# FFN blocks of two token halves with the tokens stationary, ten raw weight buffers, copies on either of two engines, and a new order

## The chip, the cores and the metric

One Trainium2 chip; the kernel runs on one of its cores. The metric is the device time of one execution in microseconds (us), the median of three runs. Engines: PE multiplies matrices (PEld is its weight load), DVE is VectorE, ACT is ScalarE, POOL is GpSimd, SP issues the DMAs.

## The reference, cut to what matters

A trunk of two layers on 256 tokens of 1024 float32 channels. Each layer has a half-weighted SwiGLU block, a mixer with an output projection, and a second SwiGLU block, each followed by a LayerNorm. The mixer of layer 0 is an RWKV-7 recurrence, that of layer 1 is stick-breaking attention; a quarter of the heads attends to a fixed memory.

```python
def swiglu(x, w_gate, w_up, w_down):          # 1024 -> 2816 -> 1024
    return (jax.nn.silu(x @ w_gate) * (x @ w_up)) @ w_down
for i in range(DEPTH):
    x = layer_norm(ALPHA * x + 0.5 * swiglu(x, ffn1...[i]))
    proj = x @ (rwkv_w_in if i % 2 == 0 else sb_w_in)
    heads = concatenate([mixer(proj[..., :]), memory_attention(proj[..., -256:])])
    x = layer_norm(ALPHA * x + heads @ w_out[i])
    x = layer_norm(ALPHA * x + 0.5 * swiglu(x, ffn2...[i]))
```

## The kernel before, in words

The 256 tokens are two halves of 128, because the two mixers run half after half, while the other half's FFN work fills PE. Every large product is done in float32r with split operands: `piece` (L599) loads a 128x1024 piece of weights into a `raw` buffer by SP's queue, ACT rounds it to `hi`, and DVE subtracts to get `lo`; `mm3` (L627) then makes three matmuls out of one (hi by hi, hi by lo, lo by hi). There are 8 `raw` buffers and 9 each of `hi` and `lo`. A piece's `raw` buffer comes free when DVE has made its `lo`.

`ffn_block` (L737) does one block of 256 of the 2816 hidden channels: four pieces of gate and up weights, two pieces of down weights. A block is either for one half (a solo block) or for both (a shared block); `LAGS`, `spread` (L1393) and the calls from L1414 say which. Of the 44 blocks of the four SwiGLUs, 18 are shared (6, 2, 7 and 3). In a solo block the transposed tokens (`xTh`, `xTl`) are stationary and 512 columns of weights move; the hidden tile `h` comes out with tokens on the partitions and is turned by two PE transposes (`to_T`, L645), with the result split by ACT and DVE into `hT`. In a shared block the weights are stationary and 256 tokens move, so that `h` comes out turned already and is split without a transpose.

The order of all work is not the program's. `Plan` (L130) records each operation, prices it (`price`, L269), and `order` (L323) puts the operations into each engine's stream by a list schedule with priorities, buffers and engine clocks; `improve` (L508) repeats this with shaken priorities and keeps the best; `issue` (L536) writes the order out. Constants at L43 to L58 and L118 to L127 set the planner (`AHEAD`, `WAIT`, `SWITCH`, `TURN`, `BOOST`) and the sequence of blocks around the mixers (`HOLD`, `TAIL`, `LAGS`).

A plain copy has a fixed engine in the program: for example `put_back` (L1124) in the RWKV mixer writes one half of a small triangular inverse by ACT and the other by DVE, `mem_attention` (L830) copies the turned scores out of PSUM by DVE, and `stick` (L1281) does the same with scores of earlier tokens and with keys and values. Names in the rows: `ps_29r` and `ps_30r` are the PSUM banks of gate and up, `ps_25r` to `ps_28r` the accumulators of the two halves, `ps_2r` and `ps_3r` the banks of transposes and small products; `T`, `Tt`, `Y`, `lb`, `L`, `Lm` are 128x768 work tiles of the mixers, `Sk` and `qr` the scores in `stick`. All rows bear L562 (L599 in the changed kernel), the line that issues them.

Of the kernel before, what the change touches and what calls it, by code (L numbers as in the profile page):

```python
# [17 lines left out]
ALU = mybir.AluOpType  # L18
# [24 lines left out]
NRAW = 8  # L43
NPIECE = 9
# [60 lines left out]
class Op:  # L105
    __slots__ = ("i", "eng", "calls", "took", "lag", "after", "opens", "closes", "pri", "func", "port", "left", "ready",
                 "end", "users", "kb", "turns", "mode", "share", "spent", "fine", "parts", "round", "places")
# [19 lines left out]
TURN = 23520.0  # L127


class Plan:  # L130
# [56 lines left out]
    def add(self, eng, fn, method, a, k):  # L187
        if self.bundle and eng == "PE":
            o = self.bundle[0]
        else:  # L190
            o = Op()
            o.i, o.eng, o.calls, o.after, o.parts = len(self.ops), eng, [], {}, []
# [13 lines left out]
        return o  # L206

    def touch(self, o, x, w):
# [16 lines left out]
        if psum:  # L225
            for q in range(q0, q1):
# [7 lines left out]
                else:  # L234
                    if st["pe"][q] is not None:
                        dep[st["pe"][q]] = True
                    for j in st["epoch"][q]:
                        if j != o.i and self.ops[j].eng != o.eng:
                            dep[j] = True
# [29 lines left out]
    def price(self, o, method, aps, a, k):  # L269
# [5 lines left out]
        n = max(free(x) for x, _ in aps)  # L275
        if o.eng == "PE":
# [13 lines left out]
        elif o.eng == "ACT":  # L290
# [3 lines left out]
            o.took = 95.0 + 0.845 * n + 93.0 * ptr + (92.0 if "accum_out" in k else 0.0)  # L294
            o.lag = 95.0
        elif o.eng == "DVE":
# [5 lines left out]
            o.took = 75.0 + n / (1.92 if fast else 0.96) + 58.0 * (ptr > 0) * (n > 1)  # L302
# [20 lines left out]
    def order(self, given=()):  # L323
# [30 lines left out]
        mode, until, busy, cold = None, WINDOW, 0.0, True  # L354
        for o in ops:
            if not o.left:
                avail[o.eng].append(o)
# [11 lines left out]
        while done < len(ops):  # L369
# [5 lines left out]
            for e, c in () if given else clock.items():  # L375
                t_e, cand = None, []
                for o in avail[e]:
# [3 lines left out]
                    t = max(t, c)  # L381
                    cand.append((t, o))
# [19 lines left out]
            t, o = min((x for x in cand if x[0] <= t_e + ahead), key=rank)  # L402
            took = o.took
# [40 lines left out]
            avail[e].remove(o)  # L444
            for j in o.users:
                u = ops[j]
                same = u.eng == e
# [8 lines left out]
                if not u.left:  # L456
                    avail[u.eng].append(u)
# [3 lines left out]
        return out, [o.users for o in ops], soft, self.reuse, [o.spent for o in ops], max(o.end for o in ops)  # L461

    def latest(self, made):

        ops = self.ops
        out, links, soft, reuse, spent, end = made
# [14 lines left out]
        for o in ops:  # L481
            if not left[o.i]:
                avail[o.eng].append(o.i)
        for _ in ops:
# [9 lines left out]
            for j in need[i]:  # L494
# [3 lines left out]
                elif p.eng == e:  # L498
                    d = start[i] - (0.0 if e in ("PE", "SP") else p.lag + AGAIN * (e != "POOL"))
                else:  # L500
                    d = start[i] - LINK - (p.lag if p.eng != "SP" else 3500.0)
                due[j] = min(due[j], d)
                left[j] -= 1
                if not left[j]:
                    avail[p.eng].append(j)
        return start

    def improve(self):  # L508
# [3 lines left out]
        kept = dict(self.buffer), self.groups  # L512
        last, fails = best, 0
        for n in range(ROUNDS):
# [12 lines left out]
            if last[-1] < best[-1]:  # L527
                best, kept, fails = last, (dict(self.buffer), self.groups), 0
# [4 lines left out]
        self.buffer, self.value = kept[0], best[-1]  # L533
        return best[0]
# [31 lines left out]
def kernel(ctx, tc, const, x, mem, f1g, f1u, f1d, f2g, f2u, f2d, ln_g, ln_b, w_out, w_mem_kv,  # L566
# [32 lines left out]
    def piece(shape, *srcs):  # L599

        n = int(np.prod(shape))
        hi = new(wp, [P, D], F32R, "hi", "hi", NPIECE)[:, :n]
        lo = new(wp, [P, D], F32R, "lo", "lo", NPIECE)[:, :n]
# [133 lines left out]
    def ffn_block(w, c, halves, beside):  # L737
        gv, uv, dv = (m.rearrange("(k p) c -> p k c", p=P) for m in w)
        fs = slice(c * FC, (c + 1) * FC)
        alone = len(halves) == 1  # L740
# [26 lines left out]
        if alone:  # L767

            hf = halves[0]
            o = ps("gu")  # L770
            for k in range(KT):
                wh, wl = gu[k // 2]
                yield mm3(o, xT[hf][0][:, k], xT[hf][1][:, k], wh[:, k % 2], wl[:, k % 2], k == 0, k == KT - 1)
            h = new(tp_, [P, FC], F32, "ta", "h", 2)
            gated(h, o[:, :FC], o[:, FC:])

            def turn_h():
                hT = new(tp_, [P, 2, 2, P], F32R, "tb", "hT", 2)
                to_T(h, (hT[:, 0], hT[:, 1]), 0, 2)
                return [down(hf, hT[:, 0], hT[:, 1])]  # L780

            return turn_h

        o = [ps("gu") for _ in range(2)]
        for k in range(KT):
            for f in range(2):
                for u in range(2):
                    wh, wl = (t[:, k % 2, u * FC + f * P:u * FC + (f + 1) * P] for t in gu[k // 2])
                    b = o[f][:, u * SEQ:(u + 1) * SEQ]
                    with nc.together():  # L790
                        nc.tensor.matmul(b, wh, xTt[0][:, k], start=k == 0 and u == 0, stop=False)
                        nc.tensor.matmul(b, wh, xTt[1][:, k], start=False, stop=False)
                        nc.tensor.matmul(b, wl, xTt[0][:, k], start=False, stop=k == KT - 1 and u == 1)
            yield
        hT = new(tp_, [P, 2, 2, SEQ], F32R, "hT", "hT", NHT)
        for f in range(2):
            h = new(tp_, [P, SEQ], F32, "ta", "h", 2)
            gated(h, o[f][:, :SEQ], o[f][:, SEQ:])
            nc.scalar.activation(hT[:, 0, f], h, AF.Copy)
            nc.vector.tensor_sub(hT[:, 1, f], h, hT[:, 0, f].bitcast(F32))  # L800
        return lambda: [down(hf, hT[:, 0, :, half_sl(hf)], hT[:, 1, :, half_sl(hf)]) for hf in halves]
# [4 lines left out]
    def memory_kv():  # L806
# [5 lines left out]
        for g in range(2):  # L812
            mT = [new(wp, [P, D], F32R, n, "mT", NPIECE).rearrange("p (s k t) -> p s k t", s=NHALF, t=P) for n in ("hi", "lo")]
# [6 lines left out]
        for hf in range(NHALF):  # L820
            mk = new(tp_, [P, MEMW], F32, "ta", "mk", 2)
            nc.scalar.activation(mk, o[hf][:, :MEMW], AF.Copy)
# [655 lines left out]
```

## Time and profile before

| what | value |
|---|---|
| median of 3 runs | 1122.68 us (1121.04 to 1122.9) |
| the profiled execution, its own time | 1121.84 us |
| span of that execution's instructions | 1120.0 us |
| PE / PEld busy in the span | 96% / 80% |
| DVE / ACT busy | 84% / 66% |
| moved by DMA | 303 MB, mean 271 GB/s |
| mean granted PE clock | 0.989 |

How to read it: PE is nearly always busy by the profile, but ends of matmuls are modelled, so the times from start to start in the timeline tell more than its busy share. The span has stages: FFN of layer 0 to about 157 us, the RWKV mixer with FFN blocks beside it to about 490, FFN of both layers to about 770, the stick-breaking mixer to about 960, and the last FFN with the last two norms.

### The profile page before, as it was taken

Reading aid. Unit: us, or ns where it says so; the run is one execution under the profiler, and the core shown is the slowest. Engines: PE = TensorE matmul, PEld = TensorE weight load, DVE = VectorE, ACT = ScalarE, POOL = GpSimd, SP = SyncE. Lnnn points to the kernel's source line nnn. Section 1 sums busy time; section 2 is a strip of 40 time slices with the busy share of each in tenths; the row PEclk is TensorE's granted clock in tenths of the full one; section 3 lists DMA queues with packets and bytes.
Section 4 is the critical chain, followed back from the end, with each engine's and each line's share of the span. In section 5 each row is a group of like instructions: output and inputs, shape, how many; then the busy total and the mean of one; then the engine's idle time right before and its main releaser. Section 6 shows DMA issues by size and latency. Waiting matters only on the chain.

```text
span 1120.0 us, 19287 instructions
## 1 busy us (share of the span) xinstructions
PE 1072.2 (96%) x7057; PEld 900.9 (80%) x7057; DVE 944.5 (84%) x1357; ACT 734.0 (66%) x979; POOL 2.7 (0%) x14
## 2 busy tenths in 40 slices
PE   7999999998899889999999999999999999999996
PEld 6888887876668668788888889898877876888885
DVE  5667679999999999998879965658899999987777
ACT  6466557884259774576766654546787799766652
POOL 0000000000000000000000000000000000000000
PEclk9999999998999999999999999999999999999999
DMA  9598769764579577899989987676987996999883
GB/s 328 181 380 283 262 195 353 247 207 146 161 239 331 177 227 226 273 329 383 309 297 325 318 296 220 189 236 213 383 296 254 334 305 226 365 364 321 269 272 115
DMA packets 212257, 303.41 MB, mean 271 GB/s; under 512 B 13844, under 2 KB 159424, under 8 KB 212162
## 3 DMA queue, kind: packets, MB, share of 16 engines
q1 hardware_dynamic: 212162, 302.18, 80.3%
q8 instruction: 55, 0.90, 0.3%
q14 instruction: 40, 0.33, 0.1%
HBM read 301.08 MB, written 1.05 MB: 270 GB/s over the span
## 4 chain that ended last, share of the span: by engine, by line
PE 58%; DVE 11%; ACT 2%; issue 2%; DMA 2%; SPq 0%; DVEq 0%; ACTq 0%
PE ps_30r L562 17%; PE ps_29r L562 17%; PE ps_27r L562 6%; PE ps_28r L562 6%; PE ps_25r L562 4%; PE ps_26r L562 4%; PE ps_3r L562 2%; PE ps_2r L562 2%; DVE x L562 1%; DVE S_104r L562 1%; ACT L562 1%; DVE lo_41r L562 1%; DVE Y_351r L562 0%; DVE lb_480r L562 0%; DVE lo_14r L562 0%
## 5 line engine op out<-in xcount | busy, mean ns | idle before, releaser
L562 ACT ACTIVATE h_32r<-ps_30r 128x256 f32<-128x256 f32 (+1 forms) x49 | 20.6, 421 | 32.7 <-PE ps_30r L562 32.5
L562 ACT ACTIVATE h_33r<-ps_29r 128x256 f32<-128x256 f32 (+1 forms) x50 | 20.6, 412 | 23.4 <-PE ps_29r L562 22.3
L562 ACT ACT_TABLE_LOAD x17 | 21.8, 1283 | 1.0 <-PEq L1466 0.7
L562 PE MATMUL ps_30r<-hi_22r,xTh 128*128 128x512 f32 x50 | 20.9, 418 | 0.0
L562 PE MATMUL ps_30r<-lo_23r,xTh 128*128 128x512 f32 x50 | 19.6, 391 | 0.0
L562 PE MATMUL ps_30r<-hi_22r,xTl 128*128 128x512 f32 x50 | 19.5, 391 | 0.0
L562 DVE TENSOR_TENSOR h_32r<-h_32r,ps_30r 128x256 f32<-128x256 f32 x31 | 12.9, 417 | 7.6 <-ACT h_32r L562 7.4
L562 ACT ACTIVATE hi_19r<-raw_12r 128x1024 fp32r<-128x1024 f32 x13 | 13.8, 1060 | 6.8 <-PE ps_28r L562 3.0
L562 DVE TENSOR_TENSOR h_33r<-h_33r,ps_29r 128x256 f32<-128x256 f32 x32 | 13.3, 416 | 5.0 <-ACT h_33r L562 4.8
L562 DVE TENSOR_TENSOR lo_20r<-raw_12r,hi_19r 128x1024 fp32r<-128x1024 f32 x13 | 15.8, 1218 | 1.7 <-DMA raw_18r<-in_ffn_w_up_dram 1.6
L562 PE MATMUL ps_29r<-hi_34r,xTh 128*128 128x512 f32 x40 | 16.4, 411 | 0.7 <-DVE h_32r L562 0.7
L562 ACT ACTIVATE hi_37r<-raw_39r 128x1024 fp32r<-128x1024 f32 x11 | 11.6, 1056 | 8.2 <-DMA raw_39r<-in_rwkv_w_in_dram 6.4
L562 PE MATMUL ps_29r<-hi_7r,xTh 128*128 128x512 f32 (+1 forms) x42 | 16.2, 386 | 0.0
L562 PE MATMUL ps_29r<-lo_35r,xTh 128*128 128x512 f32 x40 | 15.8, 394 | 0.5 <-DVE lo_35r L562 0.5
L562 ACT ACTIVATE hi_34r<-raw_21r 128x1024 fp32r<-128x1024 f32 x11 | 11.6, 1058 | 7.0 <-DMA raw_21r<-in_rwkv_w_in_dram 2.8
L562 PE MATMUL ps_29r<-hi_7r,xTl 128*128 128x512 f32 (+1 forms) x42 | 16.0, 380 | 0.0
L562 PE MATMUL ps_29r<-lo_8r,xTh 128*128 128x512 f32 (+1 forms) x42 | 16.0, 380 | 0.0
L562 PE MATMUL ps_29r<-hi_34r,xTl 128*128 128x512 f32 x40 | 15.7, 392 | 0.0
L562 PE MATMUL ps_29r<-hi_19r,xTh 128*128 128x512 f32 x38 | 15.5, 407 | 0.0
L562 PE MATMUL ps_29r<-lo_20r,xTh 128*128 128x512 f32 x38 | 15.0, 395 | 0.4 <-DVE lo_20r L562 0.4
L562 PE MATMUL ps_2r<-cst,x 128*128 128x128 f32 x48 | 8.8, 313 | 6.8 <-DMA x<-in_x_dram 5.2
L562 DVE TENSOR_TENSOR lo_35r<-raw_39r,hi_34r 128x1024 fp32r<-128x1024 f32 x10 | 12.2, 1220 | 3.6 <-ACT hi_34r L562 3.6
(1913 smaller groups left out, 4456.3 us busy)
## 6 DMA issues: line engine op xcount, KB each, us to landing
raw_9r<-in_ffn_w_down_dram SPq DMA_DIRECT2D x26, 512.0 KB, 4.8
raw_39r<-in_ffn_w_gate_dram SPq DMA_DIRECT2D x41, 256.0 KB, 4.8
raw_39r<-in_ffn_w_up_dram SPq DMA_DIRECT2D x41, 256.0 KB, 5.1
raw_12r<-in_ffn_w_gate_dram SPq DMA_DIRECT2D x38, 256.0 KB, 5.6
raw_12r<-in_ffn_w_up_dram SPq DMA_DIRECT2D x38, 256.0 KB, 4.5
raw_24r<-in_ffn_w_gate_dram SPq DMA_DIRECT2D x38, 256.0 KB, 4.3
raw_24r<-in_ffn_w_up_dram SPq DMA_DIRECT2D x38, 256.0 KB, 4.9
raw_21r<-in_ffn_w_down_dram SPq DMA_DIRECT2D x18, 512.0 KB, 4.7
```

Source lines behind the costliest of these rows:

```text
L562: fn(*[at(x) for x in a], **{n: at(x) for n, x in k.items()})
```

## The change

Four things are changed. (1) A shared block is built like a solo block: tokens stationary, 512 columns of weights moving, once for each half, then two transposes for each half. The special `hT` buffer of shared blocks goes away. (2) `raw` has 10 buffers instead of 8. (3) `nc.copy` records a plain or scaled copy with two prices, and the planner puts it on ACT, or on DVE where ACT's clock is more than `SHY` = 1000 ns later than the time at which the copy could start; a term for strided operands is added to the price. (4) The planner's constants and two block counts (`HOLD`, `TAIL`) are other ones, so that the whole order differs.

```diff
-NRAW = 8
-NPIECE = 9
+NRAW = 10
+NHI = 9
+NLO = 9
-HOLD = (3, 4)
-NHT = 1
-TAIL = (1, 2)
-AHEAD = dict(PE=100.0, DVE=200.0, ACT=0.0)
-WAIT = 7.6832
-SWITCH = 68.6
-BOOST = 12.8625
+HOLD = (2, 4)
+TAIL = (2, 2)
+AHEAD = dict(PE=0.0, DVE=200.0, ACT=0.0)
+WAIT = 10.7565
+SWITCH = 192.08
+SHY = 1000.0
+BOOST = 18.0075
...
-TURN = 23520.0
+TURN = 47040.0
...
+    def copy(self, dst, src, scale=None):
...
+        o = self.add("ACT", self.real.scalar.activation, "activation", (dst, src, AF.Copy), k, True)
+        act = o.calls, o.took, o.lag, o.port
...
+        o.ways = dict(ACT=act, DVE=([call], o.took, o.lag, o.port))
...
+                    if o.ways and e == "DVE" and clock["ACT"] <= t + SHY:
+                        continue
...
+        far = 0.9 * n * any(len(x.ap) > 1 and x.ap[-1][0] >= 16 and x.ap[-1][1] > 1 for x, _ in aps)
...
-        if alone:
...
-        o = [ps("gu") for _ in range(2)]
-        for k in range(KT):
-            for f in range(2):
-                for u in range(2):
-                    wh, wl = (t[:, k % 2, u * FC + f * P:u * FC + (f + 1) * P] for t in gu[k // 2])
-                    b = o[f][:, u * SEQ:(u + 1) * SEQ]
-                    with nc.together():
-                        nc.tensor.matmul(b, wh, xTt[0][:, k], start=k == 0 and u == 0, stop=False)
...
+        o = {hf: ps("gu") for hf in halves}
+        for k in range(KT):
+            wh, wl = (t[:, k % 2] for t in gu[k // 2])
+            for hf in halves:
+                mm3(o[hf], xT[hf][0][:, k], xT[hf][1][:, k], wh, wl, k == 0, k == KT - 1)
+            yield
...
+                to_T(hs[hf], (hT[:, 0], hT[:, 1]), 0, 2)
...
-            nc.vector.tensor_copy(turned_e[-1], pt.rearrange("p (j m t) -> p j m t", j=2, m=2))
+            nc.copy(turned_e[-1], pt.rearrange("p (j m t) -> p j m t", j=2, m=2))
...
-                nc.scalar.activation(dst[:, :, BLK * b:BLK * b + BLK], src, AF.Copy, scale=quad[:, 0:1])
-                nc.vector.tensor_scalar(dst[:, :, 32 + BLK * b:32 + BLK * b + BLK], src, quad[:, 1:2], None, ALU.mult)
+                nc.copy(dst[:, :, BLK * b:BLK * b + BLK], src, quad[:, 0:1])
+                nc.copy(dst[:, :, 32 + BLK * b:32 + BLK * b + BLK], src, quad[:, 1:2])
...
-                        nc.vector.tensor_copy(zm[:, g], z[:, :384])
+                        nc.copy(zm[:, g], z[:, :384])
```

Three places of the order that the planner makes of it follow. The first is PE at the end of the gate and up products of the first shared block. Before, with a moving operand ahead of the stationary one in each row:

```order
L562 MATMUL ps_29r<-hi_37r,xTh 128x512
L562 MATMUL ps_29r<-lo_38r,xTh 128x512
L562 MATMUL ps_29r<-hi_37r,xTl 128x512
L562 MATMUL ps_30r<-xTh,hi_16r 128x256
L562 MATMUL ps_30r<-xTl,hi_16r 128x256
L562 MATMUL ps_30r<-xTh,lo_17r 128x256
```

and now:

```order
L599 MATMUL ps_30r<-hi_16r,xTh 128x512
L599 MATMUL ps_30r<-lo_17r,xTh 128x512
L599 MATMUL ps_30r<-hi_16r,xTl 128x512
L599 MATMUL ps_2r<-cst,h_31r 128x128 x2
L599 MATMUL ps_29r<-hi_37r,xTh 128x512
L599 MATMUL ps_29r<-lo_38r,xTh 128x512
L599 MATMUL ps_29r<-hi_37r,xTl 128x512
```

In the upper rows the last three products of the shared block (bank `ps_30r`) move the tokens, 256 columns at a time, between products of the next solo block; in the lower rows the weights move there too, 512 columns at a time, and the hidden tile `h_31r` of the shared block's first half is turned by two transposes of 128 columns.

The second place is ACT at `put_back` in the first half of the RWKV mixer, where the tiles `T` and `Tt` are written for the product that PE does next. Before:

```order
L562 ACTIVATE Y_351r<-Tt_340r,cst 128x16x16
L562 ACTIVATE lb_480r<-Tt_340r,cst 128x16x16
L562 ACTIVATE hi_34r<-raw_24r 128x1024
L562 ACTIVATE bn_416r<-ps_3r 128x256
L562 ACTIVATE T_350r<-Tt_340r,cst 128x12x16 x2
L562 ACTIVATE h_33r<-ps_29r 128x256
L562 ACTIVATE hi_10r<-raw_36r 128x1024
L562 ACTIVATE Tt_340r<-Y_351r,cst 128x12x16 x2
```

and now:

```order
L599 ACTIVATE Y_369r<-Tt_358r,cst 128x16x16 x2
L599 ACTIVATE lb_498r<-Tt_358r,cst 128x16x16 x2
L599 ACTIVATE hi_37r<-raw_39r 128x1024
L599 ACTIVATE T_368r<-Tt_358r,cst 128x12x16 x4
L599 ACTIVATE h_32r<-ps_29r 128x256
L599 ACTIVATE Tt_358r<-Y_369r,cst 128x12x16 x4
```

The four copies of each of `T` and `Tt` stood two on ACT and two on DVE; now all eight stand on ACT, and so do the copies of `Y` and `lb` ahead of them.

The third place is ACT in the second half of the stick-breaking mixer, where logarithms and exponentials alternate. Before:

```order
L562 ACT_TABLE_LOAD
L562 ACTIVATE L_356r<-L_356r 128x768
L562 ACT_TABLE_LOAD
L562 ACTIVATE T_350r<-T_350r 128x768
L562 ACT_TABLE_LOAD
L562 ACTIVATE Lm_341r<-Lm_341r 128x768
L562 ACTIVATE hi_13r<-raw_21r 128x1024
L562 ACTIVATE T_350r<-T_350r 128x768
L562 ACT_TABLE_LOAD
L562 ACTIVATE h_33r<-ps_29r 128x256
L562 ACTIVATE hi_22r<-raw_18r 128x1024
L562 ACT_TABLE_LOAD
```

and now:

```order
L599 ACT_TABLE_LOAD
L599 ACTIVATE Lm_359r<-Lm_359r 128x768
L599 ACTIVATE hT_1994r<-ps_3r 128x256
L599 ACTIVATE T_368r<-Sk_373r 128x768
L599 ACT_TABLE_LOAD
L599 ACTIVATE Lm_359r<-Lm_359r 128x768
L599 ACT_TABLE_LOAD
L599 ACTIVATE T_368r<-T_368r 128x768
L599 ACT_TABLE_LOAD
L599 ACTIVATE Tt_358r<-Tt_358r 128x768
L599 ACT_TABLE_LOAD
L599 ACTIVATE h_32r<-ps_30r 128x256
```

There are 17 table loads in the whole program before and 19 now; around this place it is 6 before and 8 now.

## Rows read from the trace of the kernel before

**Rows 1.** The page's first part: each engine's busy us, share of the span and number of instructions.

```profile
PE 1072.2 (96%) x7057; PEld 900.9 (80%) x7057; DVE 944.5 (84%) x1357; ACT 734.0 (66%) x979; POOL 2.7 (0%) x14
```

**Rows 2.** Three stretches: start and end in us, length, then busy us (and instructions) of PE, PEld, DVE, ACT, POOL, granted PE clock, DMA share, GB/s. The first two are the RWKV mixer, the third is the second half of the stick-breaking mixer.

```profile
196.00:308.00 112.00, 101.00 (x1130) 82.29 (x1129) 107.42 (x215) 68.69 (x114) 0.84 (x4) 0.95 0.59 191
308.00:476.00 168.00, 156.34 (x1357) 121.18 (x1357) 165.74 (x285) 110.45 (x164) 0.20 (x1) 0.99 0.76 246
896.00:952.00 56.00, 52.93 (x298) 39.49 (x297) 52.04 (x68) 52.63 (x68) 0.00 (x0) 1.00 0.81 265
```

**Rows 3.** The page's chain that ended last, shares of the span by engine.

```profile
PE 58%; DVE 11%; ACT 2%; issue 2%; DMA 2%; SPq 0%; DVEq 0%; ACTq 0%
```

**Rows 4.** Pieces of that chain in order of time: start us, length us, what, number of instructions.

```profile
314.91 4.90 DMA raw_21r<-in_rwkv_w_in_dram
...
394.95 3.44 DMA raw_15r<-in_ffn_w_gate_dram
...
463.98 3.42 DMA raw_9r<-in_ffn_w_gate_dram
467.51 3.97 DMA raw_36r<-in_ffn_w_gate_dram
...
503.88 5.48 PE ps_30r L562 x24
...
520.17 1.08 PE ps_29r L562 x9
...
888.64 4.50 DMA raw_12r<-in_ffn_w_up_dram
```

**Rows 5.** Timeline of PE: start us, length us, instruction, out<-moving,stationary. The pair of transposes is one row.

```profile
266.96 0.39 PE L562 MATMUL ps_27r<-hi_40r,hT_527r 128*128 128x512 f32 x1
267.19 0.38 PE L562 MATMUL ps_2r<-cst,h_32r 128*128 128x128 f32 x2
267.33 0.48 PE L562 MATMUL ps_28r<-hi_40r,hT_527r 128*128 128x512 f32 x1
267.64 0.40 PE L562 MATMUL ps_28r<-lo_41r,hT_527r 128*128 128x512 f32 x1
```

**Rows 6.** Groups of DVE instructions between 157 and 490 us, by shape: count, then busy us and mean ns of one, then idle time before them.

```profile
L562 DVE TENSOR_SCALAR Lm_341r<-ps_2r 64x384 f32<-64x384 f32 x3 | 1.6, 549 | 0.0
L562 DVE TENSOR_SCALAR Y_351r<-Tt_340r,cst 128x256 f32<-128x256 f32 x4 | 1.6, 398 | 0.0
...
L562 DVE TENSOR_SCALAR Tt_340r<-Y_351r,cst 128x192 f32<-128x192 f32 x4 | 1.4, 396 | 0.0
...
L562 DVE TENSOR_SCALAR T_350r<-Tt_340r,cst 128x192 f32<-128x192 f32 x4 | 1.3, 374 | 0.0
...
L562 DVE COPY L_356r<-ps_2r 128x384 f32<-128x384 f32 x2 | 1.1, 555 | 0.1
...
L562 DVE TENSOR_SCALAR mq_339r<-ps_3r 128x256 f32<-128x256 f32 x2 | 0.8, 420 | 0.0
...
L562 DVE TENSOR_SCALAR lb_480r<-Tt_340r,cst 128x256 f32<-128x256 f32 x2 | 0.7, 346 | 0.0
...
L562 DVE COPY pT_702r<-ps_2r 128x512 f32<-128x512 f32 x1 | 0.7, 689 | 0.0
...
L562 DVE COPY pT_373r<-ps_2r 128x512 f32<-128x512 f32 x1 | 0.7, 665 | 0.0
...
L562 DVE TENSOR_SCALAR Lm_341r<-ps_3r 64x384 f32<-64x384 f32 x1 | 0.6, 561 | 0.0
```

**Rows 7.** The same between 600 and 990 us.

```profile
L562 DVE COPY Sk_355r<-ps_28r 128x384 f32<-128x384 f32 x2 | 1.1, 554 | 0.1
...
L562 DVE COPY Sk_355r<-ps_27r 128x384 f32<-128x384 f32 x2 | 1.1, 548 | 0.0
...
L562 DVE COPY eT_1711r<-ps_3r 128x512 f32<-128x512 f32 x1 | 0.7, 692 | 0.0
```

**Rows 8.** Groups of ACT instructions of the whole span, by shape, with the same columns.

```profile
L562 ACT ACTIVATE hi_19r<-raw_12r 128x1024 fp32r<-128x1024 f32 x13 | 13.8, 1060 | 6.8 <-PE ps_28r L562 3.0 <-PE ps_29r L562 2.1 <-DVE mv_266r L562 1.1
...
L562 ACT ACTIVATE T_350r<-Tt_340r,cst 128x192 f32<-128x192 f32 x4 | 2.4, 640 | 0.4 <-DVE Tt_340r L562 0.4
L562 ACT ACTIVATE Tt_340r<-Y_351r,cst 128x192 f32<-128x192 f32 x4 | 2.3, 623 | 0.0
...
L562 ACT ACTIVATE Y_351r<-ps_3r 128x384 f32<-128x384 f32 x4 | 1.9, 484 | 2.0 <-PE ps_3r L562 1.7 <-ACT hi_37r L562 0.3
...
L562 ACT ACTIVATE pT_702r<-ps_2r 128x512 f32<-128x512 f32 x3 | 1.8, 594 | 0.6 <-PE ps_2r L562 0.6
```

**Rows 9.** Waits of PE between 224 and 476 us: who waited for whom, us in total, times, longest us.

```profile
PE ps_3r L562 <- DVE x L562: 5.1, 1, 5.1
PE ps_25r L562 <- ACT Tt_340r L562: 2.9, 1, 2.9
```

**Rows 10.** One stretch of the second stick-breaking half, with the columns of Rows 2.

```profile
917.00:933.00 16.00, 15.00 (x61) 10.67 (x59) 13.65 (x18) 15.84 (x17) 0.00 (x0) 1.00 0.66 245
```

**Rows 11.** Table loads of ACT in the same stretch, with the columns of Rows 6.

```profile
L562 ACT ACT_TABLE_LOAD x6 | 7.7, 1283 | 0.1
```

**Rows 12.** Timeline of ACT at the first of them: start us, length us, instruction.

```profile
917.04 1.28 ACT L562 ACT_TABLE_LOAD   x1
918.33 0.85 ACT L562 ACTIVATE L_356r<-L_356r 128x768 f32<-128x768 f32 x1
```

More of the change, by code (lines that the diff above doesn't have):

```diff
@@ L191, in add @@
             o = Op()
[L192 removed]
+            o.i, o.eng, o.calls, o.after, o.parts, o.ways = len(self.ops), eng, [], {}, [], {} if either else None
             o.pri = o.i + self.bias
@@ L402, in order @@
             t, o = min((x for x in cand if x[0] <= t_e + ahead), key=rank)
+            for n in o.ways or (o.eng,):
+                avail[n].remove(o)
+            if o.ways:
+                self.take(o, e)
             took = o.took
@@ L443, in order @@
                     heapq.heappush(free[self.tag_of[n]], (ends[n] + LINK, self.buffer[n]))
-            avail[e].remove(o)
             for j in o.users:
                 u = ops[j]
-                same = u.eng == e
+                same = u.eng == e and not u.ways
                 if o.i in soft[j]:
@@ L460, in order @@
         out.sort(key=lambda x: (x[0], x[1]))
-        return out, [o.users for o in ops], soft, self.reuse, [o.spent for o in ops], max(o.end for o in ops)
+        return out, [o.users for o in ops], soft, self.reuse, [o.spent for o in ops], [o.eng for o in ops], \
+            max(o.end for o in ops)
     def latest(self, made):
         ops = self.ops
-        out, links, soft, reuse, spent, end = made
+        out, links, soft, reuse, spent, eng, end = made
         finish = {o.i: t + spent[o.i] for t, _, o in out}
@@ L527, in improve @@
             if last[-1] < best[-1]:
-                best, kept, fails = last, (dict(self.buffer), self.groups), 0
+                best, kept, fails = last, (dict(self.buffer), self.groups, last[-2]), 0
             else:
@@ L533, in improve @@
         self.buffer, self.value = kept[0], best[-1]
+        for o in self.ops:
+            if o.ways:
+                self.take(o, kept[2][o.i])
         return best[0]
@@ L795, in ffn_block @@
[L795 to L801, printed above, removed]
+        o = {hf: ps("gu") for hf in halves}
[4 more added lines that the diff above has]
+            yield
@@ L803, with turn_h @@
+        hs = {}
+        for hf in halves:
+            hs[hf] = new(tp_, [P, FC], F32, "ta", "h", 2)
+            gated(hs[hf], o[hf][:, :FC], o[hf][:, FC:])
+        def turn_h():
+            res = []
+            for hf in halves:
+                hT = new(tp_, [P, 2, 2, P], F32R, "tb", "hT", 2)
+                to_T(hs[hf], (hT[:, 0], hT[:, 1]), 0, 2)
+                res.append(down(hf, hT[:, 0], hT[:, 1]))
+            return res
+        return turn_h
     memKT = cp.tile([P, 2, SEQ], F32, tag="memKT", name="memKT")
```

116 lines of the change are left out of this document (59 added, 57 removed).

## The prediction

> **What bounds the kernel now.** I read the page's engine totals first, then stretches of the span, then the chain of waits, then the shapes that the change touches. The totals [rows 1] show PE at 96% and DVE at 84%, but they are an average over stages with different limits. The stretches tell them apart [rows 2]: in the RWKV mixer, from 196 to 476 us, DVE is busy 107.42 + 165.74 = 273.2 of 280 us, while PE is busy 257.3 and so has at least 22.7 us without work. In that stage DVE is the limit. In the second half of the stick-breaking mixer, 896 to 952 us, ACT (52.63 of 56) and DVE (52.04) are level, and PE stands 3.1 us. Elsewhere PE is the limit: the chain that ended last lies 58% on PE, 11% on DVE, 2% on ACT and 2% on DMA [rows 3]. The work of DVE and ACT is mostly the rounding of weights (one hi on ACT is 1.06 us [rows 8]), which the change leaves alone; what can move is the rest.
>
> The sum is made against the profiled execution, 1121.84 us. The median of the runs is 0.84 us above it, and that is added at the end.
>
> **1. Shared blocks on PE.** 18 shared blocks have 96 matmuls of 256 columns each for gate and up: 1728 become 864 of 512 columns. From start to start, 9 narrow ones take 1.08 us, 0.120 each, and 24 wide ones 5.48 us, 0.228 each [rows 4]. So 207.4 us become 197.3: 10.1 us less. New are two transposes for each half of each block, 36 pairs. In the timeline of a pair between wide matmuls, the wide one at 266.96 and the one at 267.33 take 0.68 us to the start of the next at 267.64, with the pair between them [rows 5]; two wide ones alone are 0.46, so a pair costs 0.22, and 36 pairs 7.9 us. Net **-2.2 us**, all on PE, in stages where PE is the limit. If the wide ones go at the 0.23 to 0.235 of that timeline, the 864 take 198.7 to 203.0 us and the term is -0.8 to +3.5. On ACT and DVE the block costs the same: the hidden tile is split in as many instructions of 256 columns as before, from PSUM instead of SBUF. The two hidden tiles now wait in their two buffers until they are turned, and PE has the 24 down matmuls of the block before (5.4 us) to do meanwhile, so I cost that at nothing. Without this cover PE would wait in each block for about three instructions of 256 columns out of PSUM, 0.42 each by the row of mq [rows 6], 1.3 us, and 18 times that is 23 us.
>
> **2. Copies that leave DVE.** The order shows that 48 copies go from DVE to ACT and 2 the other way; only three copies of this kind are left on DVE. That "either engine" becomes, in effect, "ACT" is read off the order, not hoped for. Between 157 and 490 us the removed ones are [rows 6] Lm 1.6 + 0.6, Y 1.6, Tt 1.4, T 1.3, L 1.1, mq 0.8, lb 0.7 and four PSUM copies of 128x512 of about 0.68 each, 2.7: 11.8 us, less about 1.0 for the two that come. So 10.8 us leave an engine that is 98% busy there. The upper bound of the gain is 10.8. The lower one is 0: the order also moves a few more lo pieces in between the same norms, and part of the PE's idle time is waiting on a dependence, not on DVE's queue. Of the two long waits of PE in that stage, the one for the norm (DVE x, 5.1 us) [rows 9] stays: between the last sum and the last scaled row of that norm, DVE's list holds the same work as before. I take a little over half, **-6 us**, since DVE's load in rows 2 is nearer to a full queue than to a free one. In the stick-breaking mixer some 8.7 us more leave DVE (the scores Sk 1.1 + 1.1, four eT of 0.68 to 0.69 [rows 7], keys, values and queries), but ACT is as full there; nothing is taken for them.
>
> Here the Trainium skill speaks against the change. "ScalarE: Activation LUTs", section "Rules for kernel authors", says that cheap arithmetic belongs on VectorE and not on ScalarE, because VectorE is faster per element. The rows agree for strided copies within SBUF (128x192: 0.640 and 0.623 us on ACT [rows 8], 0.374 and 0.396 on DVE [rows 6]) and disagree for copies out of PSUM (128x512: 0.594 on ACT, 0.689 on DVE); by the rule alone term 2 would be a loss, and the first rival below is that case.
>
> **3. Ten raw buffers.** In the chain, five DMA landings lie on the path: 4.90, 3.44, 3.42, 3.97 and 4.50 us [rows 4], 20.2 in all. A transfer can start when DVE frees a raw buffer; two more buffers let it start up to two lo splits earlier. Five times two times about 1.1 us is 11 us, the upper bound; the lower is 0, because behind a late piece mostly stands the next busy engine. I take **-2 us**: these landings are the tail of a busy DVE more than of the queue. HBM traffic does not change.
>
> **4. Table loads and ACT's queue.** Two more table loads fall into the stretch where ACT is already 15.84 of 16 us busy [rows 10], six loads of 1.283 us among it [rows 11]. Two more are 2.6 us, and the scores' chain waits behind them: **+2.6 us**. In the trace the next activation starts 0.01 us after a load ends (917.04 + 1.28, then 918.33 [rows 12]), so the row is its whole price; the bound from below is 0, if PE has block work queued. The Trainium skill, "ScalarE: Activation LUTs", section "What ACT_TABLE_LOAD costs", gives about 2.66 us for each switch, a drain included; by that the term would be +5.3. The trace shows no such drain.
>
> **5. put_back and the new order.** In each half of the RWKV mixer four more strided copies stand on ACT ahead of the product that reads T and Tt: four times about 0.6 us, 2.4 longer on ACT, 4.8 in two halves. PE already waits 2.9 us there once [rows 9]. But the new order has 48 instead of 33 wide matmuls between the last masked product and that one (first half): 15 times 0.228 is 3.4 us of cover. Together I take **-2 us**, most of the one wait; bounds -2.9 and +4.8. The other constants of the planner only act through the order and get no term.
>
> Sum: -2.2 - 6 - 2 + 2.6 - 2 = -9.6; 1121.84 - 9.6 = 1112.2, and with 0.84 for the median **1113 us**.
>
> **The rivals.** *ACT becomes the bound* (ends slower). Its queue is in order, and copies now stand behind hi pieces of 1.06 us. Against it: ACT is busy 69 and 110 us of 112 and 168 in the RWKV mixer [rows 2]. For it: 94% in the second stick-breaking half. Price: put_back uncovered 4.8, loads 2.6, four Sk copies of 0.484 and two eT of 0.594 in that half 3.1 [rows 8], 10.5 in all, and none of terms 2 and 3; with -2.2 that is +8.3, **1131 us**. It decides where ACT is busy over 95% of the stick-breaking half and PE waits for Tt more than 5 us. The rule of the Trainium skill cited under term 2 ("ScalarE: Activation LUTs", "Rules for kernel authors") would act by this mechanism.
>
> *The path was not there.* The copies were hidden behind lo pieces that PE waits for anyway, and the chain of the mixer, not DVE's load, sets the stage: only term 1 is left, -2.2, **1120.5 us**.
>
> *The stage gives all of it.* DVE's 10.8, 11 from the landings, 2.9 from the wait, 2.2 from PE, less nothing for the loads: -26.9, **1096 us**. It needs DVE to be the one limit in the RWKV mixer from end to end; that PE already lacks only 22.7 us there speaks against so much.
>
> **How the numbers follow.** A measurement of this kernel can tell about 0.2%, 2.2 us, from no change. Forecast (1106 to 1119): 0.58. ACT as bound (1123 to 1135): 0.13. No path (1118 to 1123): 0.17, of which 0.13 are the same and 0.02 each side. All of it (1091 to 1104): 0.12. Faster is 0.58 + 0.12 + 0.02 = 0.72, the same 0.13, slower 0.13 + 0.02 = 0.15. The range goes from 1099 to 1127: it leaves out the lower half of the large gain and the upper part of the ACT case, some 0.15. As both signs hold little between them, the forecast's own range is the 1106 to 1119 above.
>
> **What would show it.** Step 1: wide matmuls in shared blocks at 0.227 to 0.235 from start to start; 36 more pairs of transposes. Step 2: DVE's busy total down by some 20 us to about 925, and the stretch between the first norm and the third norm's end shorter, with PE's idle time in it below 18 us. Step 3: less than 20 us of DMA in the chain. Step 4: 19 table loads, eight in the second stick-breaking half, and that half not shorter. Step 5: PE's wait for Tt under 2 us. The prediction is wrong if the RWKV stretch keeps its length with DVE less busy, or if the time goes or comes in the pure FFN stages, where I see 2 us.

## The result, and the profile after

The changed kernel takes **1110.32 us** (median of 4 runs, 1109.82 to 1111.31), the kernel before 1122.79 (4 runs): a ratio of 0.9894, 95% interval 0.9876 to 0.9911. That is 12 us less, where 10 were forecast. The profiled execution has a span of 1108.5 us against 1120.0.

Engine totals of the changed kernel, against [rows 1]: PE is busy 4 us less, DVE 16 less, ACT 26 more.

```profile
PE 1068.3 (96%) x6265; PEld 862.6 (78%) x6265; DVE 928.6 (84%) x1312; ACT 760.0 (69%) x1027; POOL 2.7 (0%) x14
```

To see where the time went, the span is cut at points that mean the same in every order: the end of PE's last transpose behind a norm. The two stretches that matter are the whole RWKV mixer, from the first norm's transposes to the fourth's, and the second half of the stick-breaking mixer. The columns are those of [rows 2]. First the kernel before:

```profile
164.50:503.60 339.10, 316.05 (x2760) 250.77 (x2758) 329.13 (x576) 223.65 (x331) 1.04 (x5) 0.98 0.74 243
890.60:990.90 100.30, 97.23 (x505) 75.99 (x503) 94.41 (x127) 86.82 (x115) 0.00 (x0) 1.00 0.91 311
```

And the changed one:

```profile
162.30:490.40 328.10, 312.50 (x2767) 251.60 (x2766) 317.00 (x548) 237.90 (x363) 1.05 (x5) 0.98 0.76 251
876.00:980.80 104.80, 99.79 (x510) 78.13 (x509) 90.50 (x119) 92.45 (x124) 0.00 (x0) 0.97 0.84 294
```

The RWKV mixer is 11.0 us shorter with 12.1 us less on DVE; PE stands 15.6 us in it instead of 23.1. The second stick-breaking half is 4.5 us **longer**. By the same cuts the rest gives 2.2 us before the mixer, 1.4 between the two stretches (1.1 in the FFN of both layers, 0.3 in the first half of the stick-breaking mixer) and 1.4 at the end: 11.0 + 2.2 + 1.4 + 1.4 - 4.5 = 11.5, the difference of the spans.

Pieces of the chain, against [rows 4]: wide matmuls go at 5.47 / 24 = 0.228 us, and five DMA landings lie on the path inside the RWKV mixer, 16.1 us of them. They can't be set against [rows 4] as they stand: the chain of the kernel before could be followed back only to 271 us (its shares in [rows 3] add up to 75% of the span), that of the changed kernel to the start. From 271 us on the mixer has 15.7 us of landings on the path before and 6.7 now, the last two below.

```profile
218.13 2.58 DMA raw_48r<-in_ffn_w_gate_dram
239.69 3.56 DMA raw_42r<-in_ffn_w_gate_dram
256.95 3.29 DMA raw_18r<-in_w_out_dram
412.00 2.67 DMA raw_21r<-in_ffn_w_up_dram
470.71 4.00 DMA raw_24r<-in_ffn_w_up_dram
490.65 5.47 PE ps_30r L599 x24
```

PE's timeline at two pairs of transposes, against [rows 5]: from 646.91 to 647.82 are 0.91 us for two wide matmuls (0.456) and two pairs, 0.227 a pair.

```profile
646.91 0.39 PE L599 MATMUL ps_28r<-hi_7r,hT_876r 128*128 128x512 f32 x1
647.15 0.38 PE L599 MATMUL ps_3r<-cst,h_32r 128*128 128x128 f32 x2
647.36 0.38 PE L599 MATMUL ps_2r<-cst,h_31r 128*128 128x128 f32 x2
647.50 0.48 PE L599 MATMUL ps_29r<-hi_19r,xTh 128*128 128x512 f32 x1
647.82 0.40 PE L599 MATMUL ps_29r<-lo_20r,xTh 128*128 128x512 f32 x1
```

Waits of PE between 157 and 505 us, against [rows 9]: the wait for the norm has stayed (6.1 us in this wider window before), the one for Tt has shrunk from 2.9 to 0.4 us.

```profile
PE ps_2r L599 <- DVE x L599: 7.0, 2, 5.7
...
PE ps_26r L599 <- ACT Tt_358r L599: 0.4, 1, 0.4
```

The loss in the second stick-breaking half is to be read in the chain of waits, against [rows 10 to 12]:

```profile
909.68 1.28 ACT L599
...
910.97 0.84 ACT Lm_359r L599
...
911.84 1.28 ACT L599
...
913.13 0.84 ACT T_368r L599
...
913.99 1.28 ACT L599
...
915.29 0.85 ACT Tt_358r L599
...
916.16 0.96 DVE Tt_358r L599
917.12 0.47 DVE qr_408r L599
...
917.64 1.65 PE ps_2r L599 x2
```

The pieces without a name are table loads: one stands ahead of nearly every activation, since Ln (Lm, Tt) and Exp (T) alternate. DVE's add for Tt waits for the last of them; behind it in DVE's queue stands the subtraction for qr, which frees the PSUM buffer that PE wants. PE waits 5.0 us for it, and then runs at the lower of its two clock levels for a while. In the two stretches below the granted clock (third column from the end) is 0.74 while PE is nearly idle and 0.63 while it is busy again, before it is back at 1.00 (923 to 928 us).

```profile
912.00:918.00 6.00, 0.99 (x3) 0.37 (x3) 2.37 (x4) 5.91 (x7) 0.00 (x0) 0.74 0.00 0
918.00:923.00 5.00, 5.00 (x14) 3.47 (x14) 2.96 (x6) 4.11 (x5) 0.00 (x0) 0.63 0.00 0
```

Three wide matmuls of PE's timeline there stand 0.43 us apart, from start to start:

```profile
919.94 0.63 PE L599 MATMUL ps_26r<-hi_10r,hT_1994r 128*128 128x512 f32 x1
920.36 0.63 PE L599 MATMUL ps_25r<-hi_10r,hT_1994r 128*128 128x512 f32 x1
920.79 0.63 PE L599 MATMUL ps_25r<-lo_11r,hT_1994r 128*128 128x512 f32 x1
```

### The profile page after: what moved, and what is told of

Its sections match the earlier page's. It is cut to its first block, busy times and chain, and to the rows that moved or that the text cites. A ratio compares the mean times of both kernels' runs of the same rounds, so it can differ in the third digit from the quotient of the medians.

```text
span 1108.5 us, 17727 instructions
## 1 busy us (share of the span) xinstructions
PE 1068.3 (96%) x6265; PEld 862.6 (78%) x6265; DVE 928.6 (84%) x1312; ACT 760.0 (69%) x1027; POOL 2.7 (0%) x14
## 4 chain that ended last, share of the span: by engine, by line
PE 79%; DVE 11%; ACT 4%; DMA 3%; issue 2%; SPq 0%; DVEq 0%; ACTq 0%
PE ps_30r L599 25%; PE ps_29r L599 23%; PE ps_27r L599 7%; PE ps_28r L599 6%; PE ps_25r L599 6%; PE ps_26r L599 6%; PE ps_2r L599 3%; PE ps_3r L599 3%; DVE x L599 1%; DVE Y_369r L599 1%; DVE lo_44r L599 1%; DMA raw_21r<-in_ffn_w_up_dram 1%; DVE lo_17r L599 1%; ACT L599 1%; DVE lb_498r L599 1%
## 5 line engine op out<-in xcount | busy, mean ns | idle before, releaser
L599 ACT ACT_TABLE_LOAD x19 | 24.4, 1283 | 1.1 <-PEq L1488 0.7
L599 PE MATMUL ps_30r<-hi_10r,xTh 128*128 128x512 f32 (+1 forms) x60 | 23.6, 393 | 0.0
L599 PE MATMUL ps_30r<-hi_10r,xTl 128*128 128x512 f32 (+1 forms) x60 | 23.0, 383 | 0.0
L599 PE MATMUL ps_30r<-lo_11r,xTh 128*128 128x512 f32 (+1 forms) x60 | 22.9, 382 | 0.0
L599 PE MATMUL ps_29r<-hi_16r,xTh 128*128 128x512 f32 x56 | 22.8, 407 | 0.0
L599 PE MATMUL ps_30r<-hi_13r,xTh 128*128 128x512 f32 x54 | 22.0, 408 | 0.0
L599 PE MATMUL ps_29r<-hi_16r,xTl 128*128 128x512 f32 x56 | 21.9, 391 | 0.0
L599 PE MATMUL ps_29r<-lo_17r,xTh 128*128 128x512 f32 x56 | 21.9, 391 | 0.0
L599 PE MATMUL ps_30r<-lo_23r,xTh 128*128 128x512 f32 x56 | 21.8, 390 | 0.0
L599 PE MATMUL ps_30r<-lo_14r,xTh 128*128 128x512 f32 x54 | 21.2, 392 | 0.4 <-DVE lo_14r L599 0.4
L599 PE MATMUL ps_30r<-hi_13r,xTl 128*128 128x512 f32 x54 | 21.2, 393 | 0.0
L599 PE MATMUL ps_29r<-hi_10r,xTh 128*128 128x512 f32 x52 | 21.2, 408 | 0.0
```

What stands on the lines that cost most here:

```text
L599: fn(*[at(x) for x in a], **{n: at(x) for n, x in k.items()})
```

## The experiments

Two kinds of edits were made. In the first, **the order is kept**: the changed kernel's plan is made as it is, and only then one thing is altered, so that PE, SP and all other work stand in the same sequence. In the second, the planner makes a new order for the edit. All times are medians; the last column is (ratio - 0.9894) x 1122, against the changed kernel. By the intervals of the two ratios such a difference is known to about 2.4 us.

| run | order | us | ratio to before, 95% | RWKV mixer / 2nd stick half, us | against the change, us |
|---|---|---|---|---|---|
| the change | | 1110.32 | 0.9894 (0.9876 to 0.9911) | 328.1 / 104.8 | |
| copies_rwkv_back | kept | 1119.05 | 0.9974 (0.9963 to 0.9984) | 337.9 / 105.1 | +9.0 |
| copies_all_back | kept | 1121.48 | 0.9995 (0.9986 to 1.0003) | 336.3 / 107.7 | +11.3 |
| strided_back | kept | 1113.94 | 0.9928 (0.9915 to 0.9942) | 331.7 / 104.6 | +3.8 |
| raw_8 | kept | 1124.73 | 1.0024 (1.0014 to 1.0034) | 341.8 / 106.1 | +14.6 |
| shared_256 | kept | 1120.47 | 0.9992 (0.9983 to 1.0001) | 330.1 / 104.3 | +11.0 |
| ln_after_exp | all but ACT's kept | 1105.44 | 0.9853 (0.9840 to 0.9865) | 328.1 / 98.8 | -4.6 |
| copies_fixed_replanned | new | 1113.38 | 0.9922 (0.9909 to 0.9935) | 338.1 / 97.3 | +3.1 |
| raw_8_replanned | new | 1117.51 | 0.9959 (0.9947 to 0.9971) | 331.0 / 103.3 | +7.3 |
| old_planner_numbers | new | 1116.80 | 0.9950 (0.9939 to 0.9962) | 336.4 / 101.9 | +6.3 |
| shared_blocks_alone | new | 1118.03 | 0.9957 (0.9943 to 0.9971) | 336.9 / 101.2 | |
| other_seed | new | 1110.39 | 0.9894 (0.9880 to 0.9907) | 327.4 / 105.2 | 0.0 |
| loads_priced | new | 1103.59 | 0.9831 (0.9818 to 0.9845) | 328.1 / 96.5 | -7.1 |

**copies_rwkv_back, copies_all_back, strided_back.** Each copy carries the engine that it had before; after the planning, the copies go back to it. The bound 3000 on the operation's number keeps this to the RWKV mixer; copies_all_back is without it, and strided_back has a second one, that the copy writes Y, lb, T or Tt.

```diff
         for o in self.ops:
             if o.ways:
                 self.take(o, kept[2][o.i])
+        for o in self.ops:
+            if o.ways and o.i < 3000:
+                self.take(o, o.was)
```

> The changed kernel with its order kept instruction for instruction on PE, SP and in time; only the 30 copies of the RWKV mixer (and two beside it) that the change took from DVE to ACT go back to DVE at the same place in the order, and one pT copy back to ACT. Theory (DVE is the limit of that mixer, its load decides): the 10.8 us return to DVE and cost about +6 us against the changed kernel, so 1116 to 1117; bounds +3 to +11. Rival A (the gain of that mixer comes from the new order and from PE's own work, not from the engine of the copies): within 2 us of 1110. Rival B (every us of DVE counts): +10.8 or more, 1121. Seen in the trace: PE's idle time between the first norm and the transposes of the fourth goes from 15.5 us to 21 or more by the theory, stays at 15 to 17 by rival A.

> As copies_rwkv_back, and the 17 copies of the stick-breaking mixer go back to DVE as well. Theory (they were hidden, ACT being as full as DVE there): the same time as copies_rwkv_back within 2 us. Rival (DVE is the limit there too): their 8.7 us come on top in good part, +4 to +9 against copies_rwkv_back. A third way: ACT gets its 9 us back in the second stick-breaking half and that half becomes shorter, -2 to -4 against copies_rwkv_back.

> The changed kernel with its order kept and only the 14 copies within SBUF of the RWKV mixer's inverse (Y, lb, T, Tt, all but two of them strided) back on DVE, where each takes about 0.37 us in place of 0.64; the eight of put_back are among them. Theory (DVE is the limit of that mixer, so its 5.0 us more count in the share that the run copies_rwkv_back showed, 8.8 of 10.8): +3 to +5 us against the changed kernel, 1113 to 1115. Rival (these copies stand on the chain of the inverse, one behind the other on ACT, and cheap arithmetic belongs on the faster engine): -1 to -3, since put_back is 1.2 us shorter for each matrix with two engines, 1107 to 1109.

The mixer's copies cost 9.0 us, between the theory's +6 and the bound of 10.8; rival A falls. The stretch of copies_rwkv_back shows it one to one:

```profile
162.80:500.70 337.90, 316.12 (x2765) 252.79 (x2765) 328.07 (x577) 225.65 (x334) 1.05 (x5) 0.98 0.75 244
```

DVE is busy 11.1 us more and the stretch is 9.8 longer, with PE idle for 21.8 us. The copies of the stick-breaking mixer add 2.3 us, at the edge of the "same time" that was expected; PE's wait behind the table loads grows from 5.0 to 6.1. strided_back settles the rule on the faster engine. On DVE these copies are shorter, as the groups of that run show (mean ns of one behind the busy us):

```profile
L603 DVE TENSOR_SCALAR Y_369r<-Tt_358r,cst 128x256 f32<-128x256 f32 x4 | 1.6, 390 | 0.0
L603 DVE TENSOR_SCALAR Tt_358r<-Y_369r,cst 128x192 f32<-128x192 f32 x4 | 1.6, 390 | 0.0
L603 DVE TENSOR_SCALAR T_368r<-Tt_358r,cst 128x192 f32<-128x192 f32 x4 | 1.5, 386 | 0.0
L603 DVE TENSOR_SCALAR lb_498r<-Tt_358r,cst 128x256 f32<-128x256 f32 x2 | 0.7, 350 | 0.0
```

They are 5.4 us on DVE by this sum (DVE's busy time in the mixer grows by 3.9, from 317.0 to 320.9), the mixer is 3.6 us longer and the kernel loses 3.8: the engine that is slower for the single copy is the better one, because the other is full.

**raw_8.** The loads take eight buffers in turn; a load is issued only when the lo split of the piece eight places ahead of it stands in DVE's queue before it. `fewer` puts out each engine's list unchanged and holds a load back until a buffer is free.

```diff
-        return best[0]
+        return self.fewer(best, 8)
```

> The changed kernel with 8 raw buffers in place of 10 and the order of every engine kept; only each load waits for the buffer of the eighth piece before it. Theory: +2 us, 1112 (bounds 0 and +4): two buffers let a load start two lo splits earlier, and what is late then is DVE and not the queue. Rival A (no landing was bound by the buffers): 0, 1110. Rival B (the order is planned for ten buffers, and each of the mixers' stretches runs dry): +8 or more, 1118 and above, with DMA landings of over 30 us in the chain.

Rival B holds in time and sign: +14.6 us, 13.7 of them in the RWKV mixer, with 59.8 us of DMA landings in the chain from about 280 us on, where the change has 13.9. In the mixer it is 29.5 us, 24.4 of them weights, against 6.7. One of these landings shows a way that neither text had:

```profile
454.68 1.23 DVE lo_41r L632
...
456.90 5.05 DMA T_368r<-in_rwkv_lnx_g_dram
...
461.97 0.96 DVE T_368r L632
```

SP's timeline shows what the transfer of this gain, of the mixer's own norm, stood behind:

```profile
451.26 0.46 SPq L632 DMA_DIRECT2D raw_24r<-in_ffn_w_up_dram  x1
455.93 0.37 SPq L632 DMA_DIRECT2D raw_39r<-in_ffn_w_gate_dram  x1
456.35 0.46 SPq L632 DMA_DIRECT2D raw_39r<-in_ffn_w_up_dram  x1
456.90 0.43 SPq L632 DMA_DIRECT2D T_368r<-in_rwkv_lnx_g_dram  x1
```

The weight load for `raw_39r` waits 4.1 us for the lo split, and the gain, next in SP's list, goes out behind it, though DVE had read `T` for the last time by 449.7 us. DVE then waits for its landing (from the lists of SP's waits from 445 to 460 us and DVE's from 338 to 505; us in total, times, longest):

```profile
SPq L632 <- DVE lo_41r L632: 4.1, 1, 4.1
...
DVE T_368r L632 <- DMA T_368r<-in_rwkv_lnx_g_dram: 3.3, 1, 3.3
```

So DVE, the full engine, stands for a transfer that its own queue had delayed. This is one place, 3.3 of the 13.7 us; the others were not followed one by one.

**shared_256.** Each 512-column matmul of a shared block is issued as two of 256.

```diff
+                    if o.cut:
+                        out, st, mv = [at(x) for x in a]
+                        fn(out[:, :256], st, mv[:, :256], start=k["start"], stop=False)
+                        fn(out[:, 256:], st, mv[:, 256:], start=False, stop=k["stop"])
+                        continue
```

> The changed kernel with each of the 864 matmuls of 512 columns of the shared blocks' gate and up cut into two of 256 columns, at the same place in the order. Theory (PE is the limit wherever a shared block runs, and a narrow one goes each 0.120 us against 0.228): 864 x 0.012 = +10.4 us, 1120.7; by the 0.230 of other rows +8.6. Rival (the shared blocks lie in stretches where DVE or the loads set the pace): +3 or less, PE's busy share rising and its idle time falling by the rest.

The narrow ones go each 0.120 us, and +11.0 is the +10.4 of the theory. It falls where the shared blocks lie: +3.8 us before the RWKV mixer, +4.7 between the two stretches, +1.5 at the end, while the mixer and the second stick-breaking half, which have none, change by +2.0 and -0.5. PE's busy sum is 8.6 us larger and its idle time no smaller, against the rival.

```profile
699.76 0.28 PE L603 MATMUL ps_29r<-hi_40r,xTh 128*128 128x256 f32 x1
699.88 0.28 PE L602 MATMUL ps_29r<-lo_41r,xTh 128*128 128x256 f32 x1
700.00 0.28 PE L603 MATMUL ps_29r<-lo_41r,xTh 128*128 128x256 f32 x1
```

**ln_after_exp.** On ACT alone, the four Ln of the second stick-breaking half move behind the last Exp of the scores.

```diff
+        lns = [x for x in act if x[2].func == "Ln"][2:]
+        last = max(n for n, x in enumerate(act) if x[2].func == "Exp" and x[0] < lns[-1][0])
+        lines["ACT"] = [x for x in act[:last + 1] if x not in lns] + lns + [x for x in act[last + 1:] if x not in lns]
```

> The changed kernel with one thing moved: in the second half of the stick-breaking mixer the four Ln of ACT stand together behind the last Exp of the scores, in place of between them; six ACT table loads fewer, every other engine's order kept. Theory (term 4: the loads are on the path; DVE's add for Tt waits for the fifth load's Ln, and behind it in DVE's queue stands the subtraction that frees the PSUM buffer that PE waits 5.0 us for, after which PE runs some 4 us at the lower clock): the wait goes and with it the slow matmuls, -5 to -7 us against the changed kernel, 1103 to 1105. Rival (PE would only wait for the next thing there, since ACT and DVE are both full in that half): -2 us or less, 1108 to 1110.

-4.6 us (medians: -4.9), a little under the theory's -5. In ACT's timeline two loads are left of eight:

```profile
907.68 1.28 ACT L620 ACT_TABLE_LOAD   x1
908.98 0.85 ACT L620 ACTIVATE L_374r<-L_374r 128x768 f32<-128x768 f32 x1
...
911.20 0.83 ACT L620 ACTIVATE T_368r<-T_368r 128x768 f32<-128x768 f32 x1
912.04 1.28 ACT L620 ACT_TABLE_LOAD   x1
```

PE's wait for qr is 0.3 us, and the granted clock stays at 1.00 over the stretch, which is 6.0 us shorter.

**copies_fixed_replanned, raw_8_replanned, old_planner_numbers.** The planner makes a new order for each. The first lines stand in `copy`; `NRAW` is the second run; for the third, TAIL, AHEAD, WAIT, SWITCH, TURN and BOOST go back with HOLD.

```diff
+        if was == "DVE":
+            if scale is None:
+                return self.vector.tensor_copy(dst, src)
+            return self.vector.tensor_scalar(dst, src, scale, None, ALU.mult)
...
-NRAW = 10
+NRAW = 8
...
-HOLD = (2, 4)
+HOLD = (3, 4)
```

> The changed kernel with each plain copy tied to the engine it had before, and the planner made its order for that. The run copies_all_back, which kept the order made for the free choice, lost 11 us. Theory (what counts is DVE's load, 20 us more of it): +7 to +11 us, 1117 to 1121. Rival (an order made for the fixed copies hides much of them): +1 to +5, 1111 to 1115.

> The changed kernel with 8 raw buffers, and the planner made its order for 8. The run raw_8, which kept the order made for ten, lost 14 us. Theory (the ten buffers are themselves worth it, a load may start two lo splits earlier whatever the order): +8 to +14 us against the changed kernel, 1118 to 1124. Rival (it is the order that leans on them, and an order made for 8 gives most of it back): +1 to +4, 1111 to 1114.

> The changed kernel with the planner's numbers of before (HOLD, TAIL, AHEAD, WAIT, SWITCH, TURN, BOOST), so with the three parts of the change (shared blocks, copies on either engine, ten buffers) and another order. Theory (the parts make the gain and the numbers only pick among orders of like worth): within 3 us of the changed kernel, 1107 to 1113. Rival (the new order is a part of its own, as large as the others): +5 to +12, 1115 to 1122.

By the time alone copies_fixed_replanned speaks for its rival (+3.1). The stretches say otherwise:

```profile
163.00:501.10 338.10, 317.21 (x2766) 252.82 (x2765) 327.44 (x577) 226.53 (x334) 1.04 (x5) 0.98 0.74 242
886.90:984.20 97.30, 97.30 (x510) 77.29 (x508) 95.34 (x128) 82.46 (x111) 0.00 (x0) 1.00 0.93 319
```

The RWKV mixer loses 10.0 us, as with the order kept, so this new order does not hide the copies there. The second stick-breaking half wins 7.5: this order has 3 table loads in that stretch where the change has 9 (one of them outside the eight above), and ln_after_exp showed what six loads fewer are worth there, 6.0 us. So the small total is two large parts against each other; that the second is the loads alone was not tried.

raw_8_replanned gives half of raw_8 back, and +7.3 lies between its theory's +8 and its rival's +4. By stretches the new order gives back most of the loss in the mixer (2.9 us longer than the change, not 13.7) and loses 5.5 us in the stages before it and between the two stretches. old_planner_numbers follows its rival, +6.3, with 8.3 us more in the RWKV mixer and 2.9 less in the stick-breaking half (7 loads there). Its mixer shows that a smaller load on DVE is not enough:

```profile
163.60:500.00 336.40, 318.27 (x2765) 257.00 (x2765) 318.35 (x545) 237.28 (x363) 1.05 (x5) 0.97 0.75 244
```

DVE is busy 10.8 us less than in the kernel before, nearly as little as in the changed one, and yet the stretch is only 2.7 us shorter than before; PE's longest wait in it is one of 5.4 us for DVE's Y. HOLD, TAIL and the constants were put back together, so which of them counts is not shown.

**shared_blocks_alone.** The kernel before, with the block code of the change and nothing else.

> The kernel before with one part of the change alone: the shared blocks keep the tokens stationary, with two transposes for each half. 8 raw buffers, every copy on its old engine, the planner's old numbers; the planner makes the order anew. Theory (term 1: only PE's work changes, 864 x 0.024 saved and 36 pairs of transposes at 0.22 added): -2.2 us against the kernel before, bounds -5 and +3.5. Rival A (the two hidden tiles wait in their two buffers, so PE waits in each shared block): +5 to +20. Rival B (the part gives more, since a hidden tile is finished sooner): -6 to -10.

0.9957 to the kernel before, -4.8 us (-6.4 to -3.3): more than the -2.2. The profiled executions differ by 2.7 (1117.3 against 1120.0), and PE's busy sum is no smaller (1072.7 against 1072.2); by that trace it is PE's idle time that fell. By stretches, little of the 2.7 comes from where most shared blocks lie: +0.6 us before the RWKV mixer, -0.4 between the two stretches, -1.6 at the end, +0.9 in the second stick-breaking half; the mixer, which has no shared block, is 2.2 us shorter. The planner made a new order here, so the -4.8 is no clean measure of the block code, and what the 2.6 us beyond the term are stays open.

**other_seed.** `SEED = 145`.

> The changed kernel with another seed of the planner (145 in place of 144), which shakes its trial orders differently and nothing else. It shows how much one order of like kind differs from another, and so how far the runs with a new order can be read. Theory: within 3 us of the changed kernel, 1107 to 1113. Rival (each order is a draw of its own, and that of the change a lucky one): +5 us or more, 1115 and above; then copies_fixed_replanned (+3), raw_8_replanned (+7) and old_planner_numbers (+6) say nothing about their parts.

The same ratio as the change, to the last digit. It is one draw, and its order resembles the change's (its stretches are within 1 us); it says that another seed can give the same time, not that every order is as good.

**loads_priced.** The planner's list of tables no longer says that Ln and Exp share one.

```diff
-SETS = (("Exp", "Tanh"), ("Sigmoid", "Tanh"), ("Ln", "Exp"), ("Silu", "Tanh"))
+SETS = (("Exp", "Tanh"), ("Sigmoid", "Tanh"), ("Ln",), ("Silu", "Tanh"))
```

> The changed kernel with one entry of the planner's list of tables cut: Ln no longer shares one with Exp, so the planner charges the load that the trace shows at every Ln after an Exp and every Exp after an Ln. 15 table loads instead of 19, four in the second stick-breaking half instead of eight. Theory (the planner mixed Ln and Exp since it took the switches for free): the 5.0 us wait of PE goes as in the run ln_after_exp, -3 to -7 us against the changed kernel, 1103 to 1107, the rest of the order being a new draw. Rival (the new order loses elsewhere what it gains there): 1109 to 1113.

1103.59 us, the fastest of all: 0.9831 to the kernel before. PE has no idle time left in the second stick-breaking half, and the RWKV mixer keeps its 328.1 us:

```profile
163.00:491.10 328.10, 312.50 (x2766) 251.60 (x2765) 317.00 (x549) 237.79 (x363) 1.04 (x5) 0.98 0.77 251
877.20:973.70 96.50, 96.50 (x507) 76.63 (x506) 89.49 (x118) 85.40 (x119) 0.00 (x0) 1.00 0.90 314
```

## Why the prediction was right, and where its terms were off

The forecast of -9.6 us against a measured -11.5 in the profiled executions names the right place (the RWKV mixer), the right cause (DVE's load) and the right loss (table loads in the stick-breaking half). Several terms had the wrong size, and their errors went against each other, so that the sum came this near is in part luck. Of the sign against it, time that goes in the pure FFN stages, there is more than the 2 us seen there: 2.2 + 1.1 + 1.4 = 4.7. Where the part beyond the shared blocks' 2.2 comes from is not shown.

*Term 1, shared blocks (-2.2).* Its prices hold: 0.228 for a wide matmul, 0.120 for a narrow one (shared_256, +11.0 for +10.4), 0.227 for a pair. The run with the part alone gives -4.8, but with a new order, and by the traces mostly outside the stretches with most shared blocks, so the net -2.2 is confirmed by its prices and not by that run. The wait of 23 us without cover for the hidden tiles did not come.

*Term 2, copies (-6).* Mis-sized: the copies are worth 9.0 us with the order kept and 10.0 us of the mixer's stretch with a new one, close to the upper bound of 10.8. The step that was too small is the half taken for PE's waits on dependences: with the order kept, 11.1 us of DVE's load made the mixer 9.8 us longer. DVE's total of 928.6 and PE's 15.6 idle us in the stretch are as forecast (925, under 18). That the copies of the stick-breaking mixer cost nothing was off by 2 us. On DVE a strided copy takes 0.39 us, on ACT 0.62 to 0.64 [rows 8], and yet the kernel with these copies on DVE is 3.8 us slower (strided_back). The Trainium skill, "ScalarE: Activation LUTs", section "Rules for kernel authors", puts cheap arithmetic on VectorE, which it calls up to about three times faster per element in bf16. These copies are float32; the trace agrees on which engine is faster, and the run disagrees on the choice.

*Term 3, ten buffers (-2).* The worst-sized term: 7.3 us with a new order, 14.6 with the order kept, where 11 was the bound. The step that failed was the price made from five landings. First, the five are those of a chain that begins at 271 us, so "less than 20 us of DMA in the chain" had no like to compare with: the changed kernel's whole chain has 37.7 us of landings, and from 271 us on 13.9 against 20.2. Second, they were taken for the tail of a busy DVE and priced at a fifth of the bound; with eight buffers and the order kept, landings from about 280 us on grow from 13.9 to 59.8. Third, the bound left out that a blocked load holds up what stands behind it on SP, as the 3.3 us for the mixer's gain show. How the 14.6 us divide between the weights' own landings and such transfers is not shown.

*Term 4, table loads (+2.6).* Right in sign and place, too small: the half became 4.5 us longer, and the run without six of the loads gets 4.6 back. I counted the two added loads alone. What hurts is their sequence in front of Tt's add, the subtraction behind it in DVE's queue, and the clock after PE stood. A load takes 1.28 us and the next activation starts 0.01 us later, as before. The Trainium skill ("ScalarE: Activation LUTs", "What ACT_TABLE_LOAD costs") gives 2.66 us for a switch with a drain; an estimate by that figure would have made the term +5.3, nearer to the 4.5, but the trace still shows no drain.

*Term 5, put_back and the order (-2).* PE's wait for Tt is 0.4 us, as forecast. That the planner's numbers get no term of their own failed: with the old ones the change loses 6.3 us.

The terms do not add up. With the numbers or the buffers taken out, the time is that of the shared blocks alone (0.9950 and 0.9959 beside 0.9957); with the copies fixed it is 0.9922. So the gain beyond the shared blocks seems to need the ten buffers and the numbers together. That the three totals agree is no proof of it, since the stretches do not: of the mixer's 11.0 us, 2.7 are left with the old numbers, 8.1 with eight buffers and 2.2 with the shared blocks alone. These readings rest on new orders, and only the change's own was drawn twice.

The first rival (ACT as the bound) had a true part, the second stick-breaking half, and was outweighed. The path "not there" is refuted by copies_rwkv_back. That "the stage gives all of it" was near for copies and buffers, but not for the sum.

## What to carry to other kernels

When one in-order engine is about 98% busy through a stage, count most of what is taken off it as gained there (9.8 us of 11.1 here with the order kept), provided that the order can use it (2.7 of 10.8 with the old numbers), and choose the engine of a copy by who is full, not by who is faster. Price a buffer by a run with fewer of them, and look at what stands behind a blocked load in the issuing queue; before landings of two chains are compared, see from where on each chain was followed. Check an automatic planner's cost list against the trace for what it takes to be free: one entry that said Ln and Exp share a table cost more than half as much as the whole change brought.

## What the runs showed that was not expected

Each change between Ln and Exp on ACT brought a table load of 1.283 us. Eight loads begin between 904 and 926 us: two of them ahead of a hidden tile's Tanh (917.44) and of the Ln behind it, the other six where the work goes from Ln to Exp or back (copies, and one Tanh that brought no load, left aside). After PE had been busy 0.99 of 6 us, its granted clock was 0.63 over the next 5 us: wide matmuls went at 0.43 instead of 0.228 from start to start, so at the lower of the two levels, 1.2 GHz in place of 2.4. And one matmul of 512 columns cut into two of 256 with the same stationary tile costs 0.240 instead of 0.228, so that cutting alone is 5% of PE's time there.
